# Query and key transfers split in two, 128-row score products in the second attention group, a decay multiply on ScalarE

## The chip, the core and the metric

The kernel runs on one core of one Trainium2 chip. The metric is the device time of one execution in microseconds (us); three runs of the kernel before gave 2324.28, 2329.84 and 2331.13, median 2329.84. The core has five engines with queues of their own: TensorE (PE in the rows, its weight loads PEld), VectorE (DVE), ScalarE (ACT), GpSimd (POOL) and SyncE (SP). Transfers are issued from the queues of SP, POOL and ACT and carried by 16 DMA engines.

## The reference, cut to what matters

Two decoder layers on a 512 x 1024 input, each a half-step SwiGLU FFN, a token mixer with three head groups, and a second half-step FFN. All is float32. The mixer, which the change touches:

```python
aq, ak, av, bq, bk, bv, cc = split(x @ w_in[l])
o_a = diff_attention(rope(aq), rope(ak), av, lam)     # group A: two softmaxes of 32 dims per head, p0 - lam*p1
o_b = dilated_attention(rope(bq), rope(bk), bv)       # group B: 64 dims per head, three dilated windows
# group C, RWKV-7, state S of 64 x 64 per head:
#   S_t = S_{t-1} (diag(w_t) - kk_t^T (a_t*kk_t)) + v_t^T k_t ;  y_t = S_t r_t
mix = concat([o_a, o_b, o_c]) @ w_out[l]
x = layer_norm(ALPHA * x + mix)
```

## The kernel before, in words

A float32 operand is kept as two parts: hi, its rounding to the matmul's fast format, and lo, the rest; a product is the sum hi·hi + hi·lo + lo·hi. A weight thus comes in by a transfer on SP (`wr`), ScalarE makes hi (`wh`) and GpSimd subtracts lo (`wl`); there are two `wr` buffers and eight pairs of `wh` and `wl`, two parts' worth.

The FFNs are long runs of such products. Each mixer (two in all) is a set of generators ("streams"): the input projection (`columns`), the RWKV-7 steps (`decays`, `keys`, `inside`, `invert`, `scan`, `rwkv_out`), the attentions (`attend`), the output projection (`out`) and others. `Board.merge` writes one fixed order for every engine: it asks each stream when its next step could start, by a table of costs and by which buffers are free, and takes the first stream in `RANK` that is ready before the PE is free, otherwise the earliest. `Board.note` charges a transfer issued on POOL 1.04 us of that queue and its bytes at 340 KB per us plus 2 us. The engines then work through the written order, and a wait in a queue holds back all that stands behind it there.

For attention, `turner` transposes queries and keys of a head pair (names `rc`, `z`), splits them and writes hi and lo to DRAM (`qkA`, `qkB`) by SP. `fetch` brings them back by POOL, one head at a time (a "unit": pair `hp` 0 to 2, head `e` 0 or 1; six units a group and layer), into two of four `x` buffers: `q` and `k`. A unit needs its two buffers free, so the scores of two units earlier must be done. `attend` takes a unit in four query tiles `qt`: scores by the PE into bank `p`, mask, scale and row minimum on VectorE (`t`, `nm`), exponential on ScalarE, combination, transposes (`m<-kept,t`), ScalarE copy (`aT`), products with the values (`r<-v,aT`), ScalarE square (`junk`). In group A one product over 96 rows does hi·hi, lo·hi and hi·lo at once. In group B the rows 0 to 63 and 64 to 127 of `q` are the hi and lo of the query; a first product over 128 rows does both with the key's hi, a second over 64 rows does query hi with key lo.

`invert` solves the 64 x 64 triangular blocks of RWKV-7 in small products (`r<-t,x`, `r<-t16t,x`, `r<-x,t16t`) with copies between them. `scan` carries the state over eight chunks of 64 tokens: z (`r<-uv,am`, `r<-st,kr`), copied by ScalarE to `zs`; `ups` (`r<-zs,t16t`), negated into `uv`; the new state (`r<-uv,bt`), which VectorE adds to the decayed old state `sgm` to make `st`. `rwkv_out` makes y of a chunk (`m<-uv,am`, `m<-st,kr`) and normalises every two chunks into `yc`, which `mixer_tiles_c` transposes (`m<-kept,yc`) for the output projection.

Everything in the mixer that goes through the board has the line number L511 in the profile; the tile names tell the steps apart.

Of the kernel before, what the change touches and what calls it, by code (L numbers as in the profile page):

```python
# [11 lines left out]
AF = mybir.ActivationFunctionType  # L12
OP = mybir.AluOpType
# [3 lines left out]
S = 512  # L17
# [349 lines left out]
HALF = [slice(0, 64), slice(64, 128)]  # L367


class Board:  # L370
# [27 lines left out]
    def drop(self, *tiles):  # L398
        for t in tiles:
            r = self.ready[t.tensor.name]  # L400
            self.slots[r[3]].append(r[2])
            r[3] = "dropped"
# [118 lines left out]
class Mix:  # L521
# [54 lines left out]
    def u(self, name, shape=(128, S)):  # L576
        return self.get("u", name, shape)
# [191 lines left out]
    def fetch(self):  # L769

        dma = self.gps.dma_start
        ap = lambda t, off, dims: bass.AP(tensor=t.tensor, offset=t.offset + off, ap=dims)
        for grp in "AB":
            for hp in range(3):
                for e in range(2):
                    yield f"qk{grp}{hp}", "x", "x"
                    if (hp, e) == (0, 0):
                        yield f"qk{grp}{hp}", "x", "x", "bias"
                        self.bias = self.get("bias", "bias")
                        dma(self.bias, self.tr.consts[:, 130:642] if grp == "A" else self.tr.consts[:, 642:1154])  # L780
                    a = self.get("x", "q", (128, 2, S))
                    d = self.qk[grp, hp]
                    hi, lo, k = e * 64 * S, (256 + e * 64) * S, 128 * S
                    if grp == "A":
                        b = self.get("x", "k", (128, 2, S))
                        dma(a[0:64], ap(d, hi, [[256 * S, 2], [2 * S, 32], [1, 2 * S]]))
                        dma(b[0:64], ap(d, hi + k, [[0, 2], [2 * S, 32], [1, 2 * S]]))
                        dma(a[64:96], ap(d, hi, [[2 * S, 32], [1, 2 * S]]))
                        dma(b[64:96], ap(d, lo + k, [[2 * S, 32], [1, 2 * S]]))
                    else:  # L790
                        b = self.get("x", "k2", (64, S))
                        dma(a[:, 0, :], ap(d, hi, [[256 * S, 2], [S, 64], [1, S]]))
                        dma(a[:, 1, :], ap(d, hi + k, [[0, 2], [S, 64], [1, S]]))
                        dma(b, ap(d, lo + k, [[S, 64], [1, S]]))
                    self.qkt[grp, hp, e] = a.bitcast(FR), b.bitcast(FR)
                    self.mark(f"q{grp}{hp}{e}")

# [308 lines left out]
    def scan(self):  # L1106

        vec, act, pe, sp = self.vec, self.act, self.pe, self.sp
        u, drop, kr, am, bt, yt, gam = self.u, self.drop, self.kr, self.am, self.bt, self.yt, self.gam
        st = None  # L1110
        yield "yt0"
        for ch in range(8):
            hf, cc = divmod(ch, 4)
            if cc == 0:
                yield "u", "u"
                for j in range(2):
                    kr[j, hf] = u("kr", (128, 4, 2, 64))
                    sp.dma_start(kr[j, hf].rearrange("p c e t -> p (c e t)"), self.kd[j, hf])
                yield f"yt{hf}", kr[0, hf], kr[1, hf]
            yield f"uv{ch // 2}"  # L1120
            uv, vt = self.uv[ch // 2]
            uvc = uv[:, ch % 2]
            heads = [(h, h // 2, HALF[h % 2], HALF[1 - h % 2], am[hf, h % 2, cc // 2][:, cc % 2, h // 2]) for h in range(4)]
            yield ".", "r"
            z = self.acc("r", (128, 2, 64))
            for h, j, s, f, a_ in heads:
                pe.matmul(z[f, j, :], a_[s, 0:64], uvc[s, h, :], start=True, stop=st is None)
                if st is not None:
                    pe.matmul(z[f, j, :], kr[j, hf][s, cc, 0, :], st[s, j, :], start=False, stop=True)
            zs = self.t("zs", (128, 2, 64), bufs=2)  # L1130
            act.copy(zs, z)
            drop(z)
            yield ".", "r"
            ups = self.acc("r", (128, 2, 64))
            for h, j, s, f, a_ in heads:
                pe.matmul(ups[f, j, :], yt[hf][f, cc * 2 + j, :], zs[f, j, :], start=True, stop=True)
            act.mul(uvc[HALF[1], 0::2], ups[HALF[1]], -1.0)
            vec.tensor_scalar(uvc[HALF[0], 1::2], ups[HALF[0]], -1.0, None, op0=OP.mult)
            drop(ups)
            nst = None  # L1140
            if ch < 7:
                yield ".", "r", "st"
                ps = self.acc("r", (128, 2, 64))
                for h, j, s, f, a_ in heads:
                    pe.matmul(ps[s, j, :], bt[hf, cc // 2][:, cc % 2, j, s], uvc[:, h, :], start=True, stop=True)
                nst = self.get("st", "st", (128, 2, 64))
                for j in range(2):
                    gj = gam[j][:, ch:ch + 1]
                    if st is None:
                        vec.tensor_scalar(nst[:, j, :], ps[:, j, :], gj, None, op0=OP.mult)  # L1150
                    else:
                        vec.scalar_tensor_tensor(nst[:, j, :], ps[:, j, :], gj, sgm[:, j, :], op0=OP.mult, op1=OP.add)
                drop(ps)
                if ch < 6:
                    sgm = self.t("sgm", (128, 2, 64), bufs=2)
                    for j in range(2):
                        vec.tensor_scalar(sgm[:, j, :], nst[:, j, :], gam[j][:, ch + 1:ch + 2], None, op0=OP.mult)
            if cc == 3:
                drop(yt[hf], bt[hf, 0], bt[hf, 1])
            self.chunks.append((ch, uv, st, heads, kr, vt, am))  # L1160
            self.mark(f"chunk{ch}")
            st = nst
# [62 lines left out]
    def attend(self, grp):  # L1225
        tr, vec, act, pe = self.tr, self.vec, self.act, self.pe
        isA = grp == "A"
        M = 2 if isA else 1
        scale = -(32 ** -0.5 if isA else 64 ** -0.5)
        bias = None  # L1230

        def scores(x):
            hp, e, qt = x["id"]
            n = (qt + 1) * 128
            nn = max(n, 256)
            qs = slice(qt * 128, (qt + 1) * 128)
            x["l"] = self.t("l", (128, 2), bufs=8)
            x["p"] = []
            a, b = x["qk"]
            for m in range(M):  # L1240
                sc = self.acc("p1")
                if isA:
                    pe.matmul(sc[:, :nn], a[0:96, m, qs], b[0:96, m, :nn], start=True, stop=True)
                else:
                    pe.matmul(sc[:, :nn], a[:, 0, qs], a[:, 1, :nn], start=True, stop=False)
                    pe.matmul(sc[:, :nn], a[0:64, 0, qs], b[:, :nn], start=False, stop=True)
                t = self.get("t", "t")
                nm = self.t("nm", (128, 1), bufs=8)
                vec.tensor_tensor_reduce(t[:, :n], sc[:, :n], bias[:, S - n:], scale, 3e38, op0=OP.add, op1=OP.min,
                                         accum_out=nm)  # L1250
                self.drop(sc)
                act.activation(t[:, :n], t[:, :n], AF.Exp, scale=-1.0, bias=nm, accum_out=x["l"][:, m:m + 1])
                x["p"].append(t)
# [34 lines left out]
        n = len(units)  # L1288
        for i in range(n + L3):
            if i < n:  # L1290
                x = units[i]
                hp, e, qt = x["id"]
                if qt == 0:
                    if e == 0:
                        yield "o"
                        o = self.get("o", "o", (128, NT, 2, 64))
                        ss = self.t("ss" + grp, (128, 8), bufs=2)
                    yield f"q{grp}{hp}{e}", f"v{grp}{hp}"
                    bias = self.bias
                x["qk"], x["o"], x["ss"], x["v"] = self.qkt[grp, hp, e], o, ss, self.vt[grp, hp]  # L1300
                yield ("p1",) * M + ("t",) * M
                scores(x)
                if qt == NT - 1:
                    self.drop(*x["qk"])
                    if (hp, e) == (2, 1):
                        self.drop(bias)
                        if grp == "B":
                            self.mark("attended")
            if L1 <= i < n + L1:
                x = units[i - L1]  # L1310
                yield x["p"][-1], 
                combine(x)
            if L2 <= i < n + L2:
                x = units[i - L2]
                yield x["p"][0], "m", "aT"
                turn(x)
            if L3 <= i < n + L3:
                x = units[i - L3]
# [231 lines left out]
```

## Time and profile before

| | |
|---|---|
| runs | 2324.28, 2329.84, 2331.13 us |
| profiled execution | 2319.83 us, span 2318.0 us, mean granted clock 0.975 |
| PE busy | 2215.6 us (96%), PEld 1863.6 us (80%) |
| DVE, ACT, POOL busy | 1146.8 us (49%), 803.4 us (35%), 317.5 us (14%) |
| mixer of layer 0, of layer 1 | about 389 to 800 us, 1536 to 1956 us |
| the chain that ended last | PE 80%, DVE 8%, DMA 5%, issue 4% |

The PE's busy time counts a matmul for longer when the granted clock is lower, so a share of 96% is not 96% of what the PE could do. Its clock has two levels, 2.4 GHz (granted clock 1.00) and 1.2 GHz (0.50); a figure between is a mean over a stretch. The chain names at each step what released the work; a DMA on it is a transfer for which some engine waited, or that ended just when it was wanted.

### The profile page before, as it was taken

The page shows a single profiled execution, that of the slowest core. Times are in us where ns is not written, and L with a number is a line of the kernel's source. Part 1 is how long each engine was busy: PE and PEld are TensorE (multiplying, and loading weights), DVE is VectorE, ACT ScalarE, POOL GpSimd, SP SyncE. Part 2 cuts the span into 40 slices and gives each one's busy share as a digit, 9 for nine tenths or more (in the row PEclk, how much of TensorE's full clock was granted, in tenths as well). Part 3 has the DMA queues.
Part 4 walks back from the last instruction along what each step waited for, and adds up shares of the span by engine and source line. Part 5 has one row for each costly group of instructions (what it writes and reads, how often), then busy time and mean ns, then how long its engine had stood idle before and what let it go on. Part 6 is the DMA issues. An engine that isn't in the chain of part 4 may idle for free.

```text
span 2318.0 us, 31736 instructions
## 1 busy us (share of the span) xinstructions
PE 2215.6 (96%) x12384; PEld 1863.6 (80%) x12384; DVE 1146.8 (49%) x2483; ACT 803.4 (35%) x1559; POOL 317.5 (14%) x344
## 2 busy tenths in 40 slices
PE   9999999988899999999999999999878999999998
PEld 8888888787776788888888888887877867888886
DVE  3333346766566633333653332656765666333336
ACT  4322223435444323222433222343444443222222
POOL 1000002343232200000010000033432322000000
PEclk9999999999899999999999999999987999999999
DMA  5333344354433323332543333432553323233334
GB/s 171 101 102 98 113 137 146 102 136 98 104 106 101 118 74 94 98 99 91 173 120 108 101 96 109 155 128 85 136 108 94 107 95 119 84 98 91 100 109 154
DMA packets 253030, 258.34 MB, mean 111 GB/s; under 512 B 45562, under 2 KB 202304, under 8 KB 252880
## 3 DMA queue, kind: packets, MB, share of 16 engines
q1 hardware_dynamic: 221488, 228.20, 32.4%
q0 software_dynamic: 30816, 27.06, 4.8%
q8 instruction: 97, 1.59, 0.3%
q10 hardware_dynamic: 576, 1.05, 0.1%
q14 instruction: 53, 0.43, 0.1%
HBM read 233.85 MB, written 22.28 MB: 110 GB/s over the span
## 4 chain that ended last, share of the span: by engine, by line
PE 80%; DVE 8%; DMA 5%; issue 4%; POOL 1%; ACT 1%; SPq 0%; POOLq 0%; DVEq 0%; ACTq 0%
PE p L87 18%; PE p L86 18%; PE p L85 18%; PE p L511 13%; PE m L511 4%; PE r L511 3%; DMA k<-qkA 3%; PE r L86 2%; PE r L85 2%; PE r L87 2%; DMA k<-qkB 1%; DVE x L511 1%; POOL wl L511 1%; DMA q<-qkB 0%; DVE x L146 0%
## 5 line engine op out<-in xcount | busy, mean ns | idle before, releaser
L80 DVE TENSOR_TENSOR lo<-raw,hi 128x1024 fp32r<-128x1024 f32 x300 | 366.2, 1223 | 627.8 <-ACT hi L79 627.5
L87 PE MATMUL p<-xhi,lo 128*128 128x512 f32 (+1 forms) x1392 | 535.7, 385 | 0.0
L86 PE MATMUL p<-xlo,hi 128*128 128x512 f32 (+1 forms) x1392 | 533.7, 383 | 0.7 <-DVE xlo L126 0.7
L85 PE MATMUL p<-xhi,hi 128*128 128x512 f32 (+1 forms) x1392 | 533.6, 383 | 0.5 <-ACT xhi L125 0.5
L79 ACT CAST hi<-raw 128x1024 fp32r<-128x1024 f32 x300 | 315.6, 1053 | 583.5 <-PE p L86 258.1
L86 PEld LDWEIGHTS p<-xlo,hi 128*128 128x128 f32 x1392 | 261.7, 188 | 56.3 <-DVE xlo L126 1.1
L85 PEld LDWEIGHTS p<-xhi,hi 128*128 128x128 f32 x1392 | 261.8, 188 | 53.8 <-ACT xhi L125 1.0
L87 PEld LDWEIGHTS p<-xhi,lo 128*128 128x128 f32 x1392 | 261.9, 188 | 52.6
L511 POOL TENSOR_TENSOR wl<-wr,wh 128x512 fp32r<-128x512 f32 x152 | 203.8, 1360 | 670.1 <-ACT wh L511 629.3
L511 PE MATMUL p<-wh,xhi 128*128 128x256 f32 (+1 forms) x704 | 233.7, 332 | 1.4 <-DVE rb L511 1.1
L511 PE MATMUL p<-wh,xlo 128*128 128x256 f32 (+1 forms) x704 | 218.9, 311 | 0.5 <-DVE xlo L511 0.4
L511 PE MATMUL p<-wl,xhi 128*128 128x256 f32 (+1 forms) x704 | 218.5, 310 | 0.0
L87 PE MATMUL p<-hi,hl 128*128 128x512 f32 x528 | 205.8, 390 | 0.0
L86 PE MATMUL p<-lo,hh 128*128 128x512 f32 x528 | 205.8, 390 | 0.0
L85 PE MATMUL p<-hi,hh 128*128 128x512 f32 x528 | 205.7, 390 | 0.0
L511 PEld LDWEIGHTS p<-wh,xhi 128*128 128x128 f32 x704 | 138.9, 197 | 12.7 <-PE p L511 1.5
L511 PEld LDWEIGHTS p<-wh,xlo 128*128 128x128 f32 x704 | 138.7, 197 | 7.6 <-DVE xlo L511 2.2
L246 DVE TENSOR_TENSOR hr<-p,hr 128x512 f32<-128x512 f32 x88 | 60.8, 691 | 167.3 <-PE p L87 156.9
L511 PEld LDWEIGHTS p<-wl,xhi 128*128 128x128 f32 x704 | 139.2, 198 | 4.3
L247 ACT CAST hh<-hr 128x512 fp32r<-128x512 f32 x88 | 54.3, 617 | 205.9 <-DVE hr L246 195.8
L511 ACT ACTIVATE t<-t,nm 128x128 f32<-128x128 f32 (+3 forms) x144 | 80.2, 557 | 125.0 <-DVE nm L511 124.0
L85 PEld LDWEIGHTS p<-hi,hh 128*128 128x128 f32 x528 | 99.1, 188 | 20.6
(253 smaller groups left out, 3061.0 us busy)
## 6 DMA issues: line engine op xcount, KB each, us to landing
raw<-in_ffn_a_down SPq DMA_DIRECT2D x66, 512.0 KB, 3.3
raw<-in_ffn_b_down SPq DMA_DIRECT2D x66, 512.0 KB, 3.3
raw<-in_ffn_a_gate SPq DMA_DIRECT2D x44, 512.0 KB, 3.8
raw<-in_ffn_a_up SPq DMA_DIRECT2D x44, 512.0 KB, 3.9
raw<-in_ffn_b_gate SPq DMA_DIRECT2D x40, 512.0 KB, 3.9
raw<-in_ffn_b_up SPq DMA_DIRECT2D x40, 512.0 KB, 3.8
wr<-in_w_in SPq DMA_DIRECT2D x56, 256.0 KB, 3.1
wr<-in_w_in SPq DMA_DIRECT2D x24, 512.0 KB, 3.8
```

The costliest lines, as they stand in the source:

```text
L79: nc.scalar.copy(hi, raw)
L80: (vec or nc.vector).tensor_tensor(lo, raw, hi.bitcast(FT), op=OP.subtract)
L85: mm(out, lh, rh, start=first, stop=False)
L86: mm(out, lh, rl, start=False, stop=False)
L87: mm(out, ll, rh, start=False, stop=last)
L246: nc.vector.tensor_tensor(hr, acc[1, f], hr, op=OP.mult)
L247: nc.scalar.copy(hi, hr)
L511: return call(*args, **kw)
```

## The change

It has three parts.

1. `fetch`. Where one transfer had a DRAM side of three dimensions with a size of 2 outermost (query hi and lo, or the key's hi twice), there are now two transfers, one for each. In group A a unit's four transfers (two of 64 rows, 256 KB; two of 32 rows, 128 KB) become six of 32 rows, 128 KB. In group B its three (two of 128 rows, 256 KB; one of 64 rows, 128 KB) become six of 64 rows, 128 KB; the key's lo is now brought twice.
2. `attend`, group B. The second score product runs over 128 rows, not 64, so lo·lo is added.
3. `scan`. `sgm`, the state times the next chunk's decay, is made by ScalarE, not VectorE (12 instructions a layer).

```diff
                     if grp == "A":
                         b = self.get("x", "k", (128, 2, S))
-                        dma(a[0:64], ap(d, hi, [[256 * S, 2], [2 * S, 32], [1, 2 * S]]))
-                        dma(b[0:64], ap(d, hi + k, [[0, 2], [2 * S, 32], [1, 2 * S]]))
-                        dma(a[64:96], ap(d, hi, [[2 * S, 32], [1, 2 * S]]))
-                        dma(b[64:96], ap(d, lo + k, [[2 * S, 32], [1, 2 * S]]))
+                        for n, (q, r) in enumerate(((hi, hi), (lo, hi), (hi, lo))):
+                            rows = slice(32 * n, 32 * n + 32)
+                            dma(a[rows], ap(d, q, [[2 * S, 32], [1, 2 * S]]))
+                            dma(b[rows], ap(d, r + k, [[2 * S, 32], [1, 2 * S]]))
                     else:
-                        b = self.get("x", "k2", (64, S))
-                        dma(a[:, 0, :], ap(d, hi, [[256 * S, 2], [S, 64], [1, S]]))
-                        dma(a[:, 1, :], ap(d, hi + k, [[0, 2], [S, 64], [1, S]]))
-                        dma(b, ap(d, lo + k, [[S, 64], [1, S]]))
+                        b = self.get("x", "k2", (128, S))
+                        for rows, q in zip(HALF, (hi, lo)):
+                            dma(a[rows, 0, :], ap(d, q, [[S, 64], [1, S]]))
+                            dma(a[rows, 1, :], ap(d, hi + k, [[S, 64], [1, S]]))
+                            dma(b[rows], ap(d, lo + k, [[S, 64], [1, S]]))
...
                     for j in range(2):
-                        vec.tensor_scalar(sgm[:, j, :], nst[:, j, :], gam[j][:, ch + 1:ch + 2], None, op0=OP.mult)
+                        act.activation(sgm[:, j, :], nst[:, j, :], AF.Copy, scale=gam[j][:, ch + 1:ch + 2])
...
                     pe.matmul(sc[:, :nn], a[:, 0, qs], a[:, 1, :nn], start=True, stop=False)
-                    pe.matmul(sc[:, :nn], a[0:64, 0, qs], b[:, :nn], start=False, stop=True)
+                    pe.matmul(sc[:, :nn], a[:, 0, qs], b[:, :nn], start=False, stop=True)
```

The planner charges each transfer, so the written order of all engines changes from the first fetch of a layer on. Three places follow, all in layer 0.

On POOL, at the fetch of head pair 1 (`qkA_1`). Before, the two units are apart, with two subtractions for weights (`wl`) and four for the inverse (`x`) between them:

```order
L511 TENSOR_TENSOR wl<-wr,wh 128x512 x2
L511 DMA q<-qkA_1_2685 64x1x1024
L511 DMA k<-qkA_1_2685 64x1x1024
L511 DMA q<-qkA_1_2685 32x1024
L511 DMA k<-qkA_1_2685 32x1024
L511 TENSOR_TENSOR wl<-wr,wh 128x512 x2
L511 TENSOR_TENSOR x_4449<-am,table 64x256 x4
L511 DMA q<-qkA_1_2685 64x1x1024
```

Now, with the first ten of twelve transfers left out above the first row:

```order
L511 DMA q<-qkA_1_2685 32x1024
L511 DMA k<-qkA_1_2685 32x1024
L511 TENSOR_TENSOR wl<-wr,wh 128x512 x2
L511 TENSOR_TENSOR x_4578<-am,table 64x256 x4
L511 TENSOR_TENSOR wl<-wr,wh 128x512 x4
```

The twelve transfers stand in one piece, and the work that stood between the units has moved behind them.

On the PE, at the end of the first inverse (`t` and `t16t` by `x`) and before the scores of pair 1 (`k,q`). Before, the first row is followed by projection products (`wh`, `wl`), twelve of them before the last step `r<-t16t,x`; the first four are shown:

```order
L511 MATMUL r<-t_4256,x_4260 32x32 x16
L511 MATMUL p_4492<-wh,xhi 128x256
L511 MATMUL p_4492<-wl,xhi 128x256
L511 MATMUL p_4492<-wh,xlo 128x256
L511 MATMUL p_4492<-wh,xhi 128x256
```

Now the two steps of the inverse and the scores follow one another:

```order
L511 MATMUL p_4591<-wh,xlo 128x256
L511 MATMUL r<-t_4302,x_4306 32x32 x16
L511 MATMUL r<-t16t,x_4306 32x32 x16
L511 MATMUL p_4643<-k,q 128x256
L511 MATMUL p_4649<-k,q 128x256
```

The projection products have moved ahead: between the last scores of unit (0, 1) and the first of unit (1, 0) there were 24 and are now 54, and ahead of the very first scores there are 18 more than before.

## Rows read from the trace of the kernel before

**Rows 1.** Waits of the PE, whole span: us in total, times, longest us.

```profile
PE p L511 <- DMA k<-qkA: 38.7, 6, 11.5
PE m L511 <- DVE xlo L511: 10.9, 8, 1.9
...
PE r L511 <- ACT junk L511: 4.7, 4, 2.1
```

**Rows 2.** Timeline of the PE: start, length, instruction, idle time before it and releaser.

```profile
545.05 0.77 PE L511 MATMUL p<-k,q 96*128 96x256 f32 x2 [8.60 <-DMA k<-qkA]
...
630.72 0.55 PE L511 MATMUL p<-q 128*128 128x256 f32 x1 [1.23 <-DMA q<-qkB]
...
1700.71 0.77 PE L511 MATMUL p<-k,q 96*128 96x256 f32 x2 [11.54 <-DMA k<-qkA]
```

**Rows 3.** Stretches behind such waits: length, busy us by engine, granted clock, DMA.

```profile
506.02:512.00 5.98, 5.98 (x38) 5.95 (x39) 3.41 (x18) 3.16 (x12) 0.00 (x0) 0.74 0.45 69
545.05:552.00 6.95, 6.95 (x47) 6.88 (x48) 4.69 (x20) 3.05 (x12) 0.00 (x0) 0.64 0.22 68
588.54:596.00 7.46, 7.46 (x52) 6.91 (x53) 4.73 (x22) 2.89 (x12) 0.00 (x0) 0.60 0.10 28
630.72:644.00 13.28, 13.28 (x56) 9.91 (x57) 5.43 (x27) 5.46 (x18) 1.84 (x2) 0.57 0.10 30
1658.66:1664.00 5.34, 5.34 (x31) 5.30 (x32) 2.70 (x14) 2.44 (x10) 0.00 (x0) 0.68 0.46 74
1700.71:1708.00 7.29, 7.29 (x39) 7.22 (x40) 4.77 (x20) 3.20 (x12) 0.00 (x0) 0.55 0.16 53
1743.82:1756.00 12.18, 12.18 (x72) 11.50 (x73) 7.87 (x30) 5.56 (x19) 2.71 (x2) 0.54 0.06 20
1787.67:1800.00 12.33, 12.33 (x48) 9.19 (x49) 5.08 (x26) 5.05 (x16) 1.38 (x2) 0.53 0.10 33
```

**Rows 4.** Transfers by name: queue, number, KB of one, median us to landing.

```profile
q<-qkB POOLq DMA_DIRECT2D x24, 256.0 KB, 9.3
...
q<-qkA POOLq DMA_DIRECT2D x12, 256.0 KB, 12.4
...
k<-qkA POOLq DMA_DIRECT2D x12, 128.0 KB, 12.1
...
bias<-in_constants POOLq DMA_DIRECT2D x4, 256.0 KB, 3.5
...
gn<-in_c_gn_g POOLq DMA_DIRECT2D x2, 128.0 KB, 3.9
```

**Rows 5.** Timeline of POOL, issues of unit (1, 0) of group A.

```profile
526.40 0.72 POOL L511 DMA_DIRECT2D q<-qkA  x1
...
527.76 0.54 POOL L511 DMA_DIRECT2D q<-qkA  x1
```

**Rows 6.** Timeline of the PE, last two steps of the first inverse.

```profile
530.88 1.10 PE L511 MATMUL r<-t,x 64*32 64x32 f32 x32
...
534.27 1.09 PE L511 MATMUL r<-t16t,x 64*32 64x32 f32 x32 [0.68 <-ACT x L511]
```

**Rows 7.** Timeline of the PE, from y of two chunks to their transpose.

```profile
729.42 0.33 PE L511 MATMUL m<-st,kr 64*64 64x64 f32 x2
...
738.17 0.41 PE L511 MATMUL m<-kept,yc 128*128 128x128 f32 x2 [1.58 <-DVE yc L511]
```

**Rows 8.** The chain, output projection of layer 0: start, us, what.

```profile
760.52 6.99 PE p L511 x30
```

**Rows 9.** Groups by shape, PE, 640 to 700 us: count, busy us, mean ns, idle.

```profile
L511 PE MATMUL p<-k,q 64*128 64x256 f32 x6 | 2.3, 381 | 0.0
...
L511 PE MATMUL p<-q 128*128 128x256 f32 x6 | 2.2, 364 | 0.0
```

**Rows 10.** Groups by shape, VectorE and ScalarE, 480 to 760 us.

```profile
L511 DVE TENSOR_SCALAR sgm<-st,gam 128x64 f32<-128x64 f32 x12 | 4.8, 449 | 0.0
...
L511 ACT ACTIVATE uv<-r 64x128 f32<-64x128 f32 x8 | 2.2, 272 | 2.3 <-PE r L511 2.1
```

## The prediction

> **What bounds the kernel now.** The page comes first: the PE is busy for 96% of the span, so time can come only from its gaps and from stretches in which it runs at the lower clock. The list of what the PE waited for comes next, and there the reader is to see one cause far ahead of the rest: the scores of group A wait 38.7 us for their keys, in six waits, three a layer, the longest 11.5 us [rows 1]. The timeline then shows where: the PE stands 8.60 us before the scores of unit (1, 0) in layer 0 and 11.54 us in layer 1 [rows 2].
>
> A wait costs more than its length. Stretches that begin with the first product after it show a granted clock of 0.74, 0.64, 0.60 (layer 0) and 0.68, 0.55, 0.54 (layer 1) [rows 3]: part of each ran at 1.2 GHz, after an idle PE. A stretch of length L at a mean granted clock c, in which the PE was busy throughout, has done c·L of full-speed work and lost (1 − c)·L. For the six that is 1.55 + 2.50 + 2.98 + 1.71 + 3.28 + 5.60 = 17.6 us. So the waits on group A's keys and queries cost 38.7 + 17.6 = 56.3 us in all.
>
> Where group A hands over to group B, each layer has one more such place: a wait for the square `junk` (2.1 us at the longest, 4.7 us in four waits [rows 1]) and in layer 0 another 1.23 us for group B's queries [rows 2]. Behind it the clock is 0.57 and 0.53 for some 13 us [rows 3], which loses 5.7 + 5.8 us. With the idle time this is 4.7 + 1.2 + 11.5 = 17.4 us.
>
> **The transfers.** On one queue, POOL's, 256 KB for `bias` land in 3.5 us after issue and 128 KB for `gn` in 3.9 us, but 256 KB of `q<-qkA` take 12.4 and those of `q<-qkB` 9.3 [rows 4]. Size does not explain that, nor the queue. What differs is the shape: `bias` and `gn` have 128 rows outermost on both sides, the long ones a 2 on the DRAM side. The 128 KB transfers of group A have no such 2, yet take 12.1 us [rows 4]; they are issued right behind the long ones, and I read them as held up by these. So I take 3.9 us for each of the new transfers, bounded by 3.5 below and by 12.4 above. A unit of six is then ready five issues of 0.54 us [rows 5] and 3.9 us after its first issue, 6.6 us; in layer 0 unit (1, 0) was issued at 526.40 [rows 5] and used at 545.05 [rows 2], 18.7 us.
>
> The Trainium skill, "DMA: Bandwidth & Descriptors", speaks on both sides. Its section "Why a DMA increments its semaphore by 16 and not by 1" says that a transfer runs on the largest number up to 16 that divides the outermost size of both sides, which here would be 2 before and 16 now; rows 4 agree with it, as far as landing times can. Its "Rules for kernel authors" say of two transfers to separate partition halves not to bother, since they run one after the other on the same engines. By that rule the split would bring nothing but issues, which is the second rival below.
>
> Will the unit be there when wanted? The planner charges six transfers more queue time than four and therefore puts more other work ahead of the scores: 54 projection products, not 24, between units (0, 1) and (1, 0), and 18 more before the first scores (order of the PE). So the need comes later, too, while the landing comes 7 us or more earlier. Unit (1, 1) now stands in POOL's queue right behind (1, 0), ahead of two `wl`, four `x` and four more `wl`; it waits for the PE's last scores of (0, 1), and those subtractions wait behind it. The next projection part needs two of these `wl` only after the scores of (1, 0) have begun, 54 products and the inverse later, which covers the rest of the issues (six of 0.54 us) and two subtractions. I count all six group-A waits as gone: **−56.3 us**, bounds −56.3 and −18 (the landing unchanged and only the later need helping, some 3 us a wait).
>
> POOL gets 60 issues more over both layers (84 before, 144 now), about 0.6 us each or 36 us. It is busy 14% of the span; this lies beside the PE's work, unless a subtraction for weights is late.
>
> The place between the groups: in the new order more products stand there, and the last group-A steps no longer meet the inverse, but group B's first transfers still wait for the last group-A scores to free `bias`. I take half of 17.4: **−8.7 us**, bounds −17.4 and 0.
>
> **What is late next.** The moved work is missing elsewhere.
> - The first inverse: its last two products now stand without the twelve products between them. Before, the second started 534.27 − 531.98 = 2.29 us after the end of the first, and of that 0.68 us was waiting [rows 6]. Without cover the wait is up to 2.29 us, 1.6 more, and the clock may drop behind it (0 to 2.5 us, the second of the sums above). I take 3.0 a layer, bounds 0 and 4.1.
> - The last y: from the end of y (729.75) to the transpose of `yc` 8.4 us went by [rows 7]. Now 30 output products of 0.233 us [rows 8] and one transpose stand between, 7.2 us, where the last y had 57 products before. That is 1.2 us of waiting, 1.5 a layer with a little clock, bounds 0 and 4.
> - `scan` falls behind in the new order: at the start of group B two of its chunks are done, where four were. Its steps then come close together among group-B scores, with as little as three products between z and `ups` or between the state and z. The nearest rows for such a bare hand-over are the waits on `xlo`, 10.9 us in eight, 1.4 each [rows 1]. I take three a layer, 4 us, bounds 0 and 8.
> - `sgm` on ScalarE: VectorE loses 12 instructions of 0.45 us a layer [rows 10], beside the PE's work. ScalarE gets them at about 0.27 us (the `uv` row, nearest in shape [rows 10]), and each pair must now wait for VectorE's new state while exponentials and copies stand behind it. Six pairs a layer; I take 0.5 us on the path, bounds −1 and 3.
> - The 128-row product: 64 rows take 381 ns and 128 rows 364 ns at 256 columns [rows 9], so nothing, bounds ±0.
>
> Together 9 us a layer, **+18 us**.
>
> **Sum.** −56.3 − 8.7 + 18 = −47 us. The profiled execution took 2319.83 us, so on its scale 2272.8; it was 10 us quicker than the median of the runs, 2329.84. I carry the difference to the median: **2283 us**. The forecast's own bounds: −73.7 with no new waits, and −18 with every new wait at its upper bound (19 a layer, 38) and nothing at the hand-over between groups; 2256 to 2312.
>
> **Rivals.**
> 1. The gain is made and mostly given back. For it: nine VectorE and ScalarE waits of 1 to 2.7 us stand in each mixer already, and the planner's costs know nothing of a clock that drops behind them. Against it: much of the time in the group-A stretch was idle PE, not busy VectorE. With new waits at twice my figure and the clock behind them, +40 to +50: −10 us, 2320.
> 2. The split brings nothing: the landing stays near 12 us because the engines, not the shape, are the limit. For it: the DMA share is high in the first fetch (0.45 over a stretch behind the first wait [rows 3]). Against: 3.5 us for `bias` on the same queue. Then only the later need helps, 30 products more before pair 1 and 18 before the first scores at about 0.12 us, some 3 us a wait: six waits, −18, which the 18 us of new waits take back: 2330.
> 3. Slower: as rival 2, and POOL's queue blocks. The order shows that each of these transfers waits for the one eight before it on POOL. With 0.54 us an issue, the ninth comes up 4.3 us after the first; if a landing takes 12.4 us, POOL stands 8 us in each block of twelve transfers, with the weights' `wl` behind; there are three such blocks a group and layer, twelve in all. It decides from a landing of about 5 us on. If a third of 12 × 8 = 96 us reaches the PE, +32 on top of rival 2: 2362.
>
> **How the numbers follow.** Forecast 0.72; rival 1 0.13; rival 2 0.07; rival 3 0.08. About 0.3%, 7 us, is what a measurement of this kernel can tell from no change, so faster means below 2322.8. The forecast and most of rival 1 are faster: 0.72 + 0.11 = 0.83. Same: the rest of rival 1 and most of rival 2, 0.08. Slower: rival 3 and a little of rival 2, 0.09. The range reaches from the lower bound of the forecast, 2256, to 2320, rival 1's time; the forecast's own range lies inside.
>
> **What would show it.** Right: group A's and B's transfers land in 3 to 5 us; no PE wait on `qkA` over 1 us; a granted clock of 1.00 around 540 to 600 us and at the same places of layer 1; new waits of about 2 us on ScalarE's `x` copy at the end of the inverse and on `yc` near the mixer's end. Wrong: landings still near 12 us; or waits on `wl`; or the group-B stretch longer than before by what group A's has lost.

## The result, and the profile after

The changed kernel took 2273.66 us, the median of four runs (2269.21 to 2279.36); the kernel before, run beside it, 2330.49 us. The ratio is 0.9752, with an interval of 0.9716 to 0.9789: 57 us less. The forecast was 2283 us. Between the two profiled executions (2319.83 and 2273.79 us) the difference is 46 us, the sum was 47.

It is useful to split a span in two: clock times span is what it would have taken at full clock, the rest is lost to the lower clock. Before, 0.975 · 2318.0 = 2260 us and 58 lost; after, 0.980 · 2272.0 = 2227 us and 45 lost. So 33 of the 46 us are work and idle time, 13 are clock (a step of 0.001 in the clock is 2.3 us). The loss is an upper bound, since work doesn't take twice as long at 0.50: in the first run below, the product behind a 64-row score product of 256 columns started 0.51 us after it there and 0.31 us at 1.00, 1.6 times.

The waits of the PE, whole span (total us, times, longest us):

```profile
PE m L511 <- DVE xlo L511: 17.1, 6, 5.7
PE m L511 <- DVE yc L511: 4.4, 4, 1.4
...
PE p L511 <- ACT xhi L511: 4.0, 4, 1.1
PE m L511 <- DVE t L511: 3.9, 6, 1.5
PE m L511 <- ACT aT L511: 3.7, 6, 1.0
...
PE p L511 <- POOL wl L511: 3.0, 6, 0.7
PE r L511 <- ACT aT L511: 2.5, 8, 0.7
...
PE r L511 <- ACT junk L511: 1.7, 6, 0.3
```

The wait for `qkA`, 38.7 us in [rows 1], stands here no more, nor any other wait for these transfers. In its place VectorE's `xlo` leads, grown from 10.9 to 17.1 us, and GpSimd's `wl` is new. The landing times (queue, number, KB of one, median us) say why:

```profile
q<-qkB POOLq DMA_DIRECT2D x48, 128.0 KB, 4.2
q<-qkA POOLq DMA_DIRECT2D x36, 128.0 KB, 4.7
k<-qkA POOLq DMA_DIRECT2D x36, 128.0 KB, 4.8
```

Against 9.3 to 12.4 us in [rows 4]. The profile's line for POOL's queue (packets, MB, share) shows a third of the packets, 30816 before, for somewhat more bytes, and the chain no longer runs over a DMA (5% before):

```profile
q0 software_dynamic: 10656, 28.51, 4.5%
...
PE 85%; DVE 10%; ACT 3%; issue 2%; DMA 0%; POOL 0%; SPq 0%; DVEq 0%; ACTq 0%; POOLq 0%
```

Four stretches, in the columns of [rows 3] (length; busy us of PE, PEld, DVE, ACT, POOL; granted clock; DMA share; GB/s):

```profile
540.00:556.00 16.00, 13.81 (x149) 12.85 (x149) 12.57 (x35) 8.55 (x30) 5.37 (x7) 0.79 0.44 116
560.00:600.00 40.00, 38.11 (x346) 35.72 (x344) 34.21 (x119) 26.33 (x92) 15.95 (x20) 1.00 0.46 127
...
666.00:686.00 20.00, 18.47 (x102) 13.22 (x101) 9.39 (x41) 6.29 (x23) 6.17 (x12) 0.57 0.42 106
...
1794.00:1814.00 20.00, 17.48 (x121) 12.65 (x121) 10.93 (x52) 8.94 (x32) 6.17 (x12) 0.83 0.47 122
```

Group A's stretch now runs at full clock (second line), where [rows 3] had 0.60 to 0.64. The first line is the end of the inverse, the last two lie among group B's scores: there the clock still falls, in layer 0 some 35 us later than the 630 us of [rows 3]. The PE's timeline has the new waits, most of them at these falls (start, length, instruction, idle before it and releaser):

```profile
541.62 1.10 PE L511 MATMUL r<-t16t,x 64*32 64x32 f32 x32 [0.51 <-ACT x L511]
545.02 0.80 PE L511 MATMUL p<-k,q 96*128 96x256 f32 x2 [1.15 <-DVE nm L511]
...
668.29 0.79 PE L511 MATMUL p<-wh,xhi 128*128 128x512 f32 x1 [0.96 <-ACT xhi L511]
...
739.26 0.41 PE L511 MATMUL m<-kept,yc 128*128 128x128 f32 x2 [1.35 <-DVE yc L511]
...
766.85 1.97 PE L511 MATMUL m<-kept,x 128*128 128x128 f32 x8 [5.74 <-DVE xlo L511]
```

The last is the longest wait left, and nothing in the forecast speaks of it. It stands at the mixer's end, where the layer norm feeds the second FFN.

### The profile page after: what moved, and what is told of

Same layout as the page of the kernel before. It is cut to its first block, busy times and chain, and to the rows that moved or that the text cites. A ratio compares the mean times of both kernels' runs of the same rounds, so it can differ in the third digit from the quotient of the medians.

```text
span 2272.0 us, 31841 instructions
## 1 busy us (share of the span) xinstructions
PE 2197.2 (97%) x12384; PEld 1850.8 (81%) x12384; DVE 1139.2 (50%) x2459; ACT 806.2 (35%) x1583; POOL 335.5 (15%) x404
## 3 DMA queue, kind: packets, MB, share of 16 engines
q0 software_dynamic: 10656, 28.51, 4.5%
## 4 chain that ended last, share of the span: by engine, by line
PE 85%; DVE 10%; ACT 3%; issue 2%; DMA 0%; POOL 0%; SPq 0%; DVEq 0%; ACTq 0%; POOLq 0%
PE p L86 19%; PE p L87 19%; PE p L85 18%; PE p L511 15%; PE r L511 5%; PE m L511 4%; PE r L85 2%; PE r L86 2%; PE r L87 2%; DVE t L511 1%; DVE x L511 1%; ACT t L511 1%; DVE l L511 0%; DVE o L511 0%; ACT junk L511 0%
## 5 line engine op out<-in xcount | busy, mean ns | idle before, releaser
L87 PEld LDWEIGHTS p<-hi,hl 128*128 128x128 f32 x528 | 99.2, 188 | 20.5
```

What stands on the lines that cost most here:

```text
L87: mm(out, ll, rh, start=False, stop=last)
```

## The experiments

In four groups. "Order" is the order of TensorE's instructions, which the planner derives from what it believes each operation costs. Where an order is held, the planner is told the cost of one version (`charge`) while another is issued (`issue`); in the traces TensorE's products then follow one another as in that version. The kernel before took a median of 2327 to 2331 us beside all of them.

### Transfers against order

**Split transfers alone, in the planner's own order.** Part 1 of the change, with parts 2 and 3 as before:

```diff
-                            dma(b[rows], ap(d, lo + k, [[S, 64], [1, S]]))
+                        dma(b, ap(d, lo + k, [[S, 64], [1, S]]))
-act.activation(sgm[:, j, :], nst[:, j, :], AF.Copy, scale=gam...)
+vec.tensor_scalar(sgm[:, j, :], nst[:, j, :], gam..., None, op0=OP.mult)
-pe.matmul(sc[:, :nn], a[:, 0, qs], b[:, :nn], start=False, stop=True)
+pe.matmul(sc[:, :nn], a[0:64, 0, qs], b[:, :nn], start=False, stop=True)
```

> Only the first part of the change: the transfers are split, the second group-B product stays at 64 rows and sgm stays on VectorE. Theory 1 (a transfer with a 2 outermost ran on few engines, and its landing held the PE): transfers land in 4 to 5 us, no wait of the PE on qkA over 1 us, the time within 8 us of the changed kernel's 2274. Theory 3 (the decay on ScalarE or the 128-row product carries a share of the gain): slower than the changed kernel by over 10 us, 2284 or more.

**Parts 2 and 3 alone.** The old transfers, with `b` filled twice for the 128 rows. This is one transfer of 256 KB with a 2 outermost, where the kernel before has one of 128 KB without it; every run below with old transfers and 128 rows has it too:

```diff
-                        dma(b, ap(d, lo + k, [[S, 64], [1, S]]))
+                        dma(b, ap(d, lo + k, [[0, 2], [S, 64], [1, S]]))
```

> Only the second and third part: transfers as before (the key's lo now twice by one transfer with a 2 outermost), 128-row product, sgm on ScalarE. Theory 1: landing 9 to 13 us as before, PE waits on qkA of 30 us or more in total, 2325 to 2338, no difference from before. Theory 3: 2315 or less.

**Split transfers in the order of before** (64-row products, `sgm` on VectorE):

```diff
+issue(a[rows], ap(d, q, [[2 * S, 32], [1, 2 * S]]))          # what runs
+charge(a[0:64], ap(d, hi, [[256 * S, 2], [2 * S, 32], ...])) # what the planner is told
```

> The transfers are split but the planner is charged the old ones, so that the written order of every engine is that of the kernel before, apart from the issues themselves. Theory 1: landing 4 to 5 us, PE waits on qkA below 4 us in total, clock at 1.00 behind those places, 2272 to 2292. Theory 2 (the gain comes from the new order, which puts more products ahead of the scores): 2310 or more.

**Old transfers in the changed kernel's order**, the same with the roles exchanged.

> The reverse: the written order of the changed kernel on every engine, but the old transfers (a 2 outermost) are issued. Theory 1: landing 11 to 13 us; the products put ahead of the scores cover a part, so PE waits on qkA of 10 to 25 us in total, 2300 to 2330. Theory 2: 2272 to 2285, as the changed kernel.

Measured: the split alone 2349.21 us, ratio 1.0079 (1.0057 to 1.0101). It has the short landings and no wait for `qkA`, as theory 1 said, but a time in the range of theory 3, and slower than before, of which neither spoke. Parts 2 and 3 alone 2335.79 us, 1.0028 (1.0003 to 1.0054), as theory 1 said. The split in the old order 2259.08 us, 0.9683 (0.9648 to 0.9719): faster than the changed kernel and than theory 1's 2272. The old transfers in the new order 2309.17 us, 0.9900 (0.9854 to 0.9945), in theory 1's range, but with a longer landing and wait than it said.

With order and instructions of the mixer held, short landings are thus worth some 70 us in the old order and 36 in the new (there the doubled transfer of the key's lo goes, too). With the old transfers the wait is there in either order; these are the PE's list and a landing time in the new one:

```profile
PE p L511 <- DMA k<-qkA: 34.7, 6, 10.5
```

```profile
q<-qkA POOLq DMA_DIRECT2D x12, 256.0 KB, 15.8
```

The split alone has no such wait and yet loses. Its PE is not idle; it is slow (windows of the split alone):

```profile
615.00:645.00 30.00, 30.00 (x220) 24.67 (x220) 12.26 (x54) 13.55 (x43) 5.17 (x4) 0.54 0.08 28
...
684.00:721.00 37.00, 36.27 (x185) 28.01 (x185) 14.18 (x77) 14.54 (x53) 8.33 (x16) 0.53 0.23 73
```

Busy for 30.00 of 30.00 us and 36.27 of 37.00, at half speed nearly throughout. Over its span that is 0.049 · 2342.6 = 115 us lost, twice what before lost; at full clock it would by this measure take 2228 us, no more than the changed kernel.

### Which part keeps the clock up

**All parts in the order of before.** As the third experiment, with parts 2 and 3 as changed; the planner is told that `sgm` runs on VectorE.

> All three parts, but the planner is charged the old transfers and the old decay, so that TensorE's, SyncE's and (but for the decay) VectorE's and ScalarE's instructions stand in the order of the kernel before. Theory (the landing time is the whole gain, and the 128-row products and the decay on ScalarE are worth nothing of their own once the order is held): as e3_split_old_order, 2259 us, within 0.3%: 2252 to 2266, TensorE's wait rows as in e3, clock 0.985. Rival 1 (the decay on ScalarE delays the exponentials and copies queued behind it): 2267 or more, with new waits of TensorE for ScalarE's tiles aT and xhi as the changed kernel has them (12.9 us in 22 waits). Rival 2 (the 128-row products give something): below 2252.

**Split alone in the changed kernel's order.**

> Split transfers alone, with the 64-row products and the decay on VectorE, as in e1_split_alone (2349 us), but with the planner charged as in the changed kernel, so that TensorE's instructions stand in the changed kernel's order. Theory (e1 lost by its order: the clock fell to half speed for 30 to 40 us at a time where its order puts small products together): 2274 us, 2266 to 2282, clock about 0.98, no stretch of more than 20 us at half speed in the mixers. Rival (e1 lost by its instructions, the 64-row products or the decay on VectorE): 2330 or more, clock about 0.955.

**The same with 128-row products** (parts 1 and 2), and then **with the decay on ScalarE** (parts 1 and 3):

> In the changed kernel's order of TensorE: split transfers and 128-row products, the decay on VectorE. e6_split_alone_new_order (2304.6 us, neither part) and the changed kernel (2273.7 us, both parts) differ by 31 us with the same order and the same landing times. Theory (the 64-row products are what let the clock stay low: in e6 it stood at half speed for 38 us on end among group B's score products): 2274 us, 2266 to 2284, no stretch at half speed above 20 us. Rival (the decay on VectorE delays VectorE's tiles, and small waits then pull the clock down): 2295 to 2312, with the long stretches of e6.

> In the changed kernel's order of TensorE: split transfers and the decay on ScalarE, 64-row products. Theory (the 64-row products): 2295 to 2312 us, clock 0.97 or less, half speed for 30 us or more among group B's score products of each layer. Rival (the decay on VectorE): 2274 us, 2266 to 2284.

**Parts 2 and 3 without the split, in the order of before.**

> The kernel before with 128-row products and the decay on ScalarE, the transfers' outermost dimensions and TensorE's order left as before. Theory (the parts add: the split is worth 2330 to 2259 us in this order, and the two other parts 2259 to 2245 with the split): some 14 us less than before, 2316 us, 2308 to 2325, with the waits for k of qkA at 34 us or more. Rival (the two parts bring something only where no transfer is late): 2323 or more, no different from before.

**All parts in the order of the split alone.**

> All three parts in TensorE's order of e1_split_alone (2349 us, 115 us of its span lost to the lower clock). In the changed kernel's order the 128-row products were worth 23 to 30 us (e6 and e10 against e9 and the changed kernel), in the order of the kernel before 14 at most (e3 against e5). Theory (the products over 64 rows are most of what e1 lost, whatever the order): 2320 us or less, clock 0.965 or more, no stretch of 30 us at half speed among group B's score products. Rival (e1's order itself is the loss, because it puts little between those products): 2335 or more, with the long stretches of e1 still there.

Medians in us, by order and parts (the last column is the profiled span's loss to the clock, as above):

| transfers | order | 64 rows, VectorE | 128 rows, ScalarE | lost, us |
|---|---|---|---|---|
| old | before's | 2330 | 2328.47 (0.9995; 0.9966 to 1.0024) | 58, 60 |
| split | before's | 2259.08 | 2245.45 (0.9637; 0.9603 to 0.9671) | 34, 20 |
| split | changed | 2304.56 (0.9892; 0.9853 to 0.9931) | 2273.66 | 71, 45 |
| split | split alone's | 2349.21 | 2295.94 (0.9855; 0.9822 to 0.9888) | 115, 57 |

For the third row's first number the loss is that of a run with a span of 2302.5 us at 0.969. In the changed order the parts singly: 128-row products with the decay on VectorE 2280.32 us (2276.90 to 2287.64), 64-row products with the decay on ScalarE 2303.22 (2297.84 to 2317.88). So the decay's place is worth 1 to 7 us, within what the runs spread, and the 64 rows are what costs 24 to 30. All parts in the order of before came out below 2252, as its second rival said. The split alone in the changed order, at 2304.56, lies between its theory and its rival: both the order and the instructions count.

Much of that is the products' own time. Rows by shape over the whole span, first the split in the old order, then all parts in it (count, busy us, mean ns), all at a granted clock of 1.00:

```profile
L511 PE MATMUL p<-k,q 64*128 64x256 f32 x24 | 9.1, 381 | 0.0
L511 PE MATMUL p<-q 128*128 128x256 f32 x24 | 8.8, 367 | 0.0
```

```profile
L511 PE MATMUL p<-q 128*128 128x256 f32 x24 | 8.5, 359 | 0.0
...
L511 PE MATMUL p<-k,q 128*128 128x256 f32 x24 | 6.7, 281 | 0.0
```

381 ns become 281. With the products of 384 and 512 columns the sum of these rows falls from 41.9 to 34.4 us. But rows may overlap, so the distance from start to start says more. One pair of scores and the product behind it, with the weight loads of the second and third (PEld), in the same two runs:

```profile
678.96 0.36 PE L511 MATMUL p<-q 128*128 128x256 f32 x1
679.25 0.38 PE L511 MATMUL p<-k,q 64*128 64x256 f32 x1
679.56 0.50 PE L511 MATMUL p<-wh,xhi 128*128 128x512 f32 x1
...
679.25 0.18 PEld L511 LDWEIGHTS p<-k,q 64*128 64x128 f32 x1
679.56 0.19 PEld L511 LDWEIGHTS p<-wh,xhi 128*128 128x128 f32 x1
```

```profile
670.02 0.37 PE L511 MATMUL p<-q 128*128 128x256 f32 x1
670.23 0.28 PE L511 MATMUL p<-k,q 128*128 128x256 f32 x1
670.34 0.39 PE L511 MATMUL p<-wh,xhi 128*128 128x512 f32 x1
...
670.10 0.19 PEld L511 LDWEIGHTS p<-k,q 128*128 128x128 f32 x1
670.23 0.19 PEld L511 LDWEIGHTS p<-wh,xhi 128*128 128x128 f32 x1
```

With 64 rows each of these loads begins only with its product, and the pair takes 0.60 us; with 128 they begin 0.13 and 0.11 us ahead, beside the product before, and the pair takes 0.32. Added up from the traces over the 48 pairs, waits taken off, it is 35.5 against 20.8 us: 14.7 of the 17.7 us between the two spans. In the changed order it is 37.7 against 20.1, of 28.5 us between the spans, though ten of the 64-row pairs there ran at the lower clock.

Most of the rest is the clock. The same stretch of the mixer (1802 to 1856 us), in the changed order, with 64 rows and the decay on ScalarE; with 128 rows and the decay on VectorE; and with both as in the changed kernel, which differs from the first by the rows alone:

```profile
1802.00:1856.00 54.00, 52.73 (x239) 40.52 (x240) 20.67 (x102) 20.86 (x73) 8.36 (x16) 0.51 0.28 88
```

```profile
1802.00:1856.00 54.00, 49.44 (x306) 36.98 (x305) 31.27 (x139) 22.96 (x78) 14.54 (x22) 0.81 0.35 108
```

```profile
1802.00:1856.00 54.00, 49.73 (x344) 36.98 (x342) 34.38 (x144) 23.69 (x81) 11.64 (x17) 0.97 0.32 99
```

In all three the clock falls at the start of group B's scores after waits of about 1 us or less. With 128 rows it rises soon, and may fall again; with 64 it stays down for 50 us although the PE is busy for 52.73 of 54. That is layer 1; in layer 0 the same run with 64 rows was down for 17 us only, where 30 had been expected of each layer. And in the order of the split alone, the two stretches shown above, with all parts:

```profile
615.00:645.00 30.00, 29.87 (x372) 26.22 (x371) 19.26 (x81) 18.12 (x62) 6.91 (x8) 1.00 0.26 73
...
684.00:721.00 37.00, 33.16 (x195) 25.62 (x195) 25.45 (x107) 17.11 (x58) 8.69 (x12) 0.92 0.29 108
```

1.00 and 0.92 instead of 0.54 and 0.53, and 53 us less in all, as expected of the 64 rows; the rival, that the order itself loses it, fails for the larger part. But the order keeps its share: with all parts, the three orders still stand 2245, 2274 and 2296 us apart, at 2219 to 2232 us of full-clock time. Without the split the 128 rows bring nothing, as the rival of that run had it. Its waits say at least part of why: the doubled transfer of the key's lo is a long one, and the PE's waits on group B's transfers rise from 2.3 us before to 13.0, which takes back 10.7 of the 12.5 us that the pairs save there by the same count (37.3 to 24.8).

```profile
PE p L511 <- DMA q<-qkB: 7.6, 4, 3.9
PE p L511 <- DMA k<-qkB: 5.4, 3, 2.3
```

### What makes a transfer long

> The changed kernel with its order of TensorE, VectorE and ScalarE held and two kinds of transfer exchanged. Group A's high and low halves come in pairs again, source dimensions 2 x 32 x 512, but cut in two along the free dimension, so 128 KB each with an outermost dimension of 2. Group B's first 64 rows of queries and keys come in one transfer of 256 KB, source dimensions 64 x 2 x 512, outermost dimension 64. Theory (the outermost dimension sets how long a transfer takes to land): the 128 KB transfers of outermost 2 land in 6 us or more, some in 9 and above, TensorE's waits for k of qkA are back at 10 us or more in all; the 256 KB transfer of outermost 64 lands in less than 6 us. Rival (the size does): 128 KB lands in 4.2 to 4.8 us whatever its dimensions, no wait for qkA, and the 256 KB transfer takes 8 us or more.

```diff
+for m in range(2):                                           # group A, 128 KB, outermost 2
+    issue(a[0:64, m], ap(d, hi + m * S, [[256 * S, 2], [2 * S, 32], [1, S]]))
+    issue(b[0:64, m], ap(d, hi + k + m * S, [[0, 2], [2 * S, 32], [1, S]]))
+issue(a[64:96], ap(d, hi, [[2 * S, 32], [1, 2 * S]]))         # b[64:96] likewise
+issue(a[rows], ap(d, hi, [[S, 64], [128 * S, 2], [1, S]]))   # group B, 256 KB, outermost 64
```

```profile
q<-qkA POOLq DMA_DIRECT2D x36, 128.0 KB, 7.7
k<-qkA POOLq DMA_DIRECT2D x36, 128.0 KB, 7.9
q<-qkB POOLq DMA_DIRECT2D x12, 256.0 KB, 4.8
```

```profile
PE p L511 <- DMA k<-qkA: 5.2, 3, 4.0
```

The outermost dimension makes a transfer slow, the size alone doesn't: 128 KB with a 2 outermost takes 7.7 and 7.9 us, 256 KB with 64 outermost 4.8. Where a 2 is outermost the size seems to count as well: 256 KB took 15.8 us in the same order, shown above. How the 2 does it no run shows. Fewer engines at work would fit, but POOL's queue also moved 21216 packets here against 10656, and neither can be told from the other. Of the 36 in a row, 12 have 32 outermost and wait behind the others: they land in 7.4 us at the median, against 4.7 where all have 32. The waits came back smaller than the theory said (5.2 us in three, not 10), and the only execution timed took 2276.58 us, no different from the changed kernel: at 8 us the landing is still mostly hidden in this order.

### The wait at the mixer's end

> The changed kernel with TensorE's order held and the last 8 gate and up subtractions of each layer on VectorE instead of GpSimd. Theory (VectorE's two-operand steps of the layer norm, 0.68 to 0.70 us each elsewhere, took 1.1 to 2.3 us because GpSimd subtracted beside them, and so TensorE waited 5.7 us for xlo at the end of each mixer): those steps back at 0.7 us, the wait at 3 us or less in each layer, the stretch at half speed behind it shorter: 2262 to 2270 us. Rival (the layer norm's chain is as long as that by itself, and VectorE now has 8 subtractions more before it): the wait 5.7 us or more, 2274 to 2282 us.

```diff
-LOPOOL = lambda i: True
+LOPOOL = lambda i: i < 34      # from there on VectorE subtracts; the planner is told GpSimd
```

Timeline of VectorE and GpSimd in the changed kernel, then of VectorE and the PE in this one:

```profile
759.20 3.44 DVE L511 SCALAR_TENSOR_TENSOR x<-x,mv,gb 128x512 f32<-128x512 f32 x2
...
758.54 6.44 POOL L511 TENSOR_TENSOR wl<-wr,wh 128x512 fp32r<-128x512 f32 x4 [1.80 <-ACT wh L511]
```

```profile
758.49 1.41 DVE L511 SCALAR_TENSOR_TENSOR x<-x,mv,gb 128x512 f32<-128x512 f32 x2
...
767.05 1.97 PE L511 MATMUL m<-kept,x 128*128 128x128 f32 x8 [3.90 <-DVE xlo L511]
```

1.72 us for one such step beside GpSimd's subtractions, 0.70 without. The mechanism is right, and the Trainium skill has it ("SBUF — State Buffer", "Who interferes with whom": a VectorE instruction with two inputs in SBUF contends with a GpSimd instruction that reads SBUF). But the wait only fell from 5.74 to 3.90 us, not to 3, and the time stayed: 2275.35 us (2273.36 to 2276.84). VectorE now has the eight subtractions itself, in the same stretch.

## Why the prediction was right, point by point

The number was right to 10 us, and its main step held. That it came so near is in part luck: the total also rests on two effects that the sum had at nothing or not at all, and that nearly cancelled. Its upper end of 2312 us also leaves out the bound of −18 that it gave to the first term; with that it would be 2350.

- **Landing.** Taken as 3.9 us, measured 4.2 to 4.8; the cause, the 2 outermost, is shown by the exchange of shapes. The rule of the Trainium skill on which it leaned ("DMA: Bandwidth & Descriptors", "Why a DMA increments its semaphore by 16 and not by 1") agrees with these rows, as far as landing times can show. The Trainium skill's "Rules for kernel authors", on the same page, against two transfers to separate partition halves do not hold here, where each half has more rows outermost than the whole had: 2330 to 2259 us with the order held. So the second and third rivals, both with long landings, did not come about.
- **Six waits, 38.7 us.** All gone, as forecast. Their clock, 17.6 us by the same upper bound, can't be told apart in the changed kernel, whose whole gain in clock is 13 us; the order of before shows more, 58 to 34 us lost.
- **Between the groups, −8.7.** The waits went (`junk` 4.7 to 1.7 us, `q<-qkB` to nothing), the low clock moved: it cost 11.5 us behind the hand-over of [rows 3] and costs (1 − 0.57) · 20 + (1 − 0.83) · 20 = 12.0 us in the two stretches shown above. Some 4 us gained, half of what was forecast.
- **New waits, +18.** The inverse: 0.51 us for ScalarE's `x`, where up to 2.29 were feared, but 1.15 and 0.53 us right behind it, and a low clock worth (1 − 0.79) · 16 = 3.4 us: 5.6 us in layer 0, above the 3.0 taken and its bound of 4.1. `yc`: 3.2 to 4.4 us in all, less than half of the 3 taken. Bare hand-overs: 8 us were taken for `scan`, but no wait on its `zs` or `uv` stands in the list. In its place `xhi`, `t` and `aT`, of the projections and attentions, came to 14.1 us in the rows above against 3.9 before; that the sizes are close is luck. A sign of being wrong also showed, waits on `wl`, but at 3.0 us in six it is small.
- **The mixer's end.** Not in the sum: idle time of 1.42 + 1.09 + 1.83 us there became 5.74, 1.4 us more. The 6.2 us by which the waits for `xlo` grew over both layers mostly replace others.
- **The 128-row product, ±0: the step that failed.** I compared 381 ns with 364 in [rows 9]. But the 364 belong to the first product of the pair, which still takes 359 when the second has 128 rows too; the second then takes 281. And rows were compared, not starts: the pair went from 0.60 to 0.32 us. A bound of nothing also left out the clock. In the changed order this part is worth 24 to 30 us: without it the change would have come to 2303 us.
- **The order.** I read from it which products stand where, and took it as moving waits only. Held against the order of before with all else equal, it costs 2274 − 2245 = 28 us, some 10 of it idle time of the PE (added up from the two traces), most of the rest clock. This is the first rival's mechanism, a gain mostly given back in waits and clock; in full it appears in the split alone, 2349 us, where the 64 rows were left in.

So the change is two gains and a loss: the split some 70 us in the order of before, the 128 rows and the decay 14 more, the planner's new order −28. All three parts without the new order make the best kernel here, 2245.45 us (2238.29 to 2247.38).

## What to carry to other kernels

Read the outermost size of a slow transfer before its bytes, and cut it so that rows, not a 2, stand outermost. Where a planner places work by costs, hold its order in one experiment and its instructions in another: here one edit, the split, was worth some −70 us or +20 depending on the order alone. Multiply span by granted clock for each version; if the products agree (2219 to 2236 us for all with short landings), what is left is mostly clock, and small products are to be looked at, not waits. Compare products from start to start, not by the length of their rows: some 15 us were hidden there.

## What had not been expected of the hardware

TensorE stayed at 1.2 GHz for 27 to 55 us on end with hardly any idle time, among short products (0.40 and 0.44 us for 64 and 128 columns at that clock, in the split alone) with 64-row products between them. Where these had 128 rows, the longest such stretch of a mixer was 17 us. It takes the order, too: with the split and 64 rows in the order of before, 10 us was the longest. The Trainium skill ("TensorE: Matmul & The Clock Gate", "Part 1: The HAM clock gate") says that the lower clock is the default and that activity releases it; the row with 52.73 of 54 us busy at 0.51 does not fit that if a busy PE is meant. But busy here goes by the length of rows, and the pair above fills 0.60 us with rows for what takes 0.32 us with 128 rows. No run here tells whether the 64 rows, or the changes between 64 and 128 rows, are what counts.

A product over 64 rows that alternates with one over 128 took longer, 381 ns, than the same over 128 rows, 281 ns, and in the rows above neither its weights nor those of the 128-row product behind it were loaded ahead, while both were where all had 128 rows.
